# One level of Strassen for the second layer's input projection, with the weight sums made in DRAM

## The chip, the cores and the metric

One core of a Trainium2 chip. The metric is the device time of one execution in microseconds (us), the median of several runs. TensorE (PE) multiplies matrices, VectorE (DVE) and ScalarE (ACT) work elementwise, GpSimd (POOL) does a little of this and issues DMAs, SyncE (SP) issues most DMAs.

## The reference

Two residual layers over x of 512 tokens by 2048 columns, in float32:

```python
def hybrid_layer(x, ...):               # layer 0
    h = rms_norm(x, norm_g)
    aq, ak, av, agate, alog_in, bq, bk, bv, bgate = split_cols(h @ w_in, IN0_SIZES)
    ya = mixer_a(...)                   # gated delta rule in chunks of 64, both directions
    yb = mixer_b(bq, bk, bv, bgate, ...)  # attention with rotary positions
    return x + jnp.concatenate([ya, yb], axis=-1) @ w_out

def gmlp_layer(x, ...):                 # layer 1
    h = rms_norm(x, norm_g)
    u, v, gate = jnp.split(h @ w_in, 3, axis=-1)      # w_in is 2048 x 6144
    u = gelu(u)
    v = layer_norm(gelu(v), ln_g, ln_b)
    s = jnp.einsum('gts,bnsgc->bntgc', w_s, vc) + bias   # vc: v in 4 chunks, 16 column groups
    z = u * s * silu(gate)
    return x + z @ w_out
```

## The kernel before

Every large product is split into float32r parts: an operand is hi + lo, and a product is hi x hi + hi x lo + lo x hi, three matmuls into one PSUM bank. `proj` (L244) makes one group of up to 512 weight columns: 16 k-steps (128 rows of the weights each), in each of them four parts (blocks of 128 tokens or columns), in each part three matmuls. A part is a quarter-step below.

Weights come in slabs of 256 rows (512 KB) by `load_raw` (L213) on SP's queue into three buffers `raw`, and `split` (L222) makes hi on ScalarE (L230) and lo on VectorE (L231), two k-steps ahead of the matmuls that use them; a slab is asked for when the first half of the slab two before it is split, so it has four k-steps to land.

All engines run in the order in which the program is written out. That order comes from a small planner: `sub` (L170) is called once per quarter-step, counts the waits of side work down by `tick` and lets the lanes `front`, `back` and `side` write out pieces of their generators. A generator yields a positive number for VectorE time that it asks for, and a negative one for quarter-steps to wait. `force` runs the lanes until a named key is done. `spill` queues a store for some quarter-steps later. A group of 512 columns is 64 quarter-steps, one of 352 columns is counted as 44.

The groups in order: A2, K0, K1, Q0, Q1, V0, BQ0, V1, BQ1, BKV, A0, A1, BG0, BG1 (layer 0's input), O0 to O3 (its output), VV0 to VV3 (layer 1's v), GG0, UU0, ..., GG3, UU3 (gate and u), R0 to R3 (layer 1's output). Beside K0 to V1 runs `batch` (L530): it makes the decays, loads the gram blocks into M (six loads on POOL's queue, L629), inverts the triangular blocks of 32 in M and W on VectorE (L660 to L666), and hands the off-diagonal blocks to `merge` (L758), 256 small matmuls a direction, whose inputs go through DRAM (e_d, then eb) by POOL's queue. Four scattered stores (L703) put the diagonal blocks into u_d. `chunk_a` sets the key "A2" when the decayed query blocks are stored; then the recursion `scan` (L810) and `attention` start.

The last output group of layer 0 leaves x1; `h1_turn` (L1277) transposes it and makes h1 (hi and lo). The sums of squares become the row scale rs1, applied at evacuation. v stays in SBUF (vt), is normalised in place by `layer_norm1` (L1322), and `spatial` (L1359), one for each pair GGj, UUj, splits it by column groups, multiplies by the spatial weights, combines with u x gate and transposes to zT. `z_split` makes the output projection's operand of it.

## Time and profile before

| | |
|---|---|
| runs, median of 3 | 1748.71 us (1745.74 to 1748.79) |
| profiled execution: its time, its span | 1745.44 us, 1743.7 us |
| TensorE busy in the span | 1714.5 us (98%) |
| VectorE, ScalarE, POOL busy | 866.1, 698.4, 152.5 us |
| layer 1's input stage | 1002 to 1556 us |
| moved by DMA | 221 MB |

The busy time of TensorE is counted from the start of matmuls that overlap; a part without idle time is not a part at full speed, so the spacing of starts is read where a matmul's price is wanted.

### The profile page before, as it was taken

Reading aid. Unit: us, or ns where it says so; the run is one execution under the profiler, and the core shown is the slowest. Engines: PE = TensorE matmul, PEld = TensorE weight load, DVE = VectorE, ACT = ScalarE, POOL = GpSimd, SP = SyncE. Lnnn points to the kernel's source line nnn. Section 1 sums busy time; section 2 is a strip of 40 time slices with the busy share of each in tenths; the row PEclk is TensorE's granted clock in tenths of the full one; section 3 lists DMA queues with packets and bytes.
Section 4 is the critical chain, followed back from the end, with each engine's and each line's share of the span. In section 5 each row is a group of like instructions: output and inputs, shape, how many; then the busy total and the mean of one; then the engine's idle time right before and its main releaser. Section 6 shows DMA issues by size and latency. Waiting matters only on the chain.

```text
span 1743.7 us, 23347 instructions
## 1 busy us (share of the span) xinstructions
PE 1714.5 (98%) x8819; PEld 1402.7 (80%) x8819; DVE 866.1 (50%) x1570; ACT 698.4 (40%) x1423; POOL 152.5 (9%) x177
## 2 busy tenths in 40 slices
PE   9999999979999999999999999999999999999999
PEld 9877777757788997788788888888888888888887
DVE  4545588825765767875533333238342424245232
ACT  6443443514445555565532232223333433343221
POOL 0200200230001313440100000000000000000000
PEclk9999999989999999999999999999999999999999
DMA  6534544695556555435444453333333233333443
GB/s 199 134 103 124 125 121 104 160 185 141 144 141 172 158 145 178 129 105 169 151 133 129 128 166 97 90 92 107 98 91 90 81 96 92 96 115 113 134 139 103
DMA packets 166560, 221.36 MB, mean 127 GB/s; under 512 B 48545, under 2 KB 77521, under 8 KB 166448
## 3 DMA queue, kind: packets, MB, share of 16 engines
q1 hardware_dynamic: 161952, 207.27, 41.1%
q0 software_dynamic: 3744, 11.75, 3.2%
q8 instruction: 69, 1.13, 0.3%
q10 hardware_dynamic: 752, 0.86, 0.2%
q14 instruction: 43, 0.35, 0.1%
HBM read 186.18 MB, written 33.65 MB: 126 GB/s over the span
## 4 chain that ended last, share of the span: by engine, by line
PE 71%; ACT 3%; DVE 3%; issue 2%; DMA 2%; POOL 0%; SPq 0%; ACTq 0%; DVEq 0%
PE acc L276 19%; PE acc L275 19%; PE acc L277 19%; PE acc L271 2%; PE acc L273 2%; PE acc L272 2%; PE su L881 1%; PE sc L850 1%; DVE wlo L231 1%; PE sc L877 1%; ACT whi L230 1%; DMA eb<-e_d 1%; PE sc L863 1%; PE sc L851 1%; PE at L84 1%
## 5 line engine op out<-in xcount | busy, mean ns | idle before, releaser
L231 DVE TENSOR_TENSOR wlo<-raw,whi 128x512 fp32r<-128x512 f32 (+1 forms) x544 | 373.6, 687 | 747.8 <-ACT whi L230 740.2
L230 ACT CAST whi<-raw 128x512 fp32r<-128x512 f32 (+1 forms) x544 | 330.3, 608 | 724.8 <-PE acc L277 543.1
L275 PE MATMUL acc<-whi,h1h 128*128 128x512 f32 x768 | 304.5, 396 | 0.0
L277 PE MATMUL acc<-whi,h1l 128*128 128x512 f32 x768 | 303.3, 395 | 0.0
L276 PE MATMUL acc<-wlo,h1h 128*128 128x512 f32 x768 | 303.3, 395 | 0.0
L271 PE MATMUL acc<-hTh,whi 128*128 128x512 f32 x512 | 211.4, 413 | 0.9 <-DVE cs L509 0.9
L273 PE MATMUL acc<-hTh,wlo 128*128 128x512 f32 x512 | 203.2, 397 | 1.6 <-issue 1.6
L272 PE MATMUL acc<-hTl,whi 128*128 128x512 f32 x512 | 202.9, 396 | 0.0
L277 PEld LDWEIGHTS acc<-whi,h1l 128*128 128x128 f32 x768 | 143.9, 187 | 35.2
L275 PEld LDWEIGHTS acc<-whi,h1h 128*128 128x128 f32 x768 | 144.0, 187 | 34.8
L276 PEld LDWEIGHTS acc<-wlo,h1h 128*128 128x128 f32 x768 | 144.0, 188 | 34.5
L275 PE MATMUL acc<-whi,hTh 128*128 128x352 f32 (+1 forms) x384 | 160.7, 418 | 0.0
L277 PE MATMUL acc<-whi,hTl 128*128 128x352 f32 (+1 forms) x384 | 137.8, 359 | 0.2 <-DVE hTl L351 0.2
L276 PE MATMUL acc<-wlo,hTh 128*128 128x352 f32 (+1 forms) x384 | 137.9, 359 | 0.0
L273 PEld LDWEIGHTS acc<-hTh,wlo 128*128 128x128 f32 x512 | 96.5, 188 | 25.2 <-issue 2.0
L271 PEld LDWEIGHTS acc<-hTh,whi 128*128 128x128 f32 x512 | 96.8, 189 | 21.4 <-DVE cs L509 1.5
L272 PEld LDWEIGHTS acc<-hTl,whi 128*128 128x128 f32 x512 | 97.0, 190 | 18.6
L275 PE MATMUL acc<-whi,zh 128*128 128x512 f32 x224 | 87.2, 389 | 0.0
L276 PE MATMUL acc<-wlo,zh 128*128 128x512 f32 x224 | 86.9, 388 | 0.0
L277 PE MATMUL acc<-whi,zl 128*128 128x512 f32 x224 | 86.9, 388 | 0.0
L277 PEld LDWEIGHTS acc<-whi,hTl 128*128 128x128 f32 x384 | 72.1, 188 | 9.3 <-DVE hTl L351 0.5
L275 PEld LDWEIGHTS acc<-whi,hTh 128*128 128x128 f32 x384 | 72.8, 190 | 6.0 <-ACT hTh L350 0.3
(318 smaller groups left out, 2384.5 us busy)
## 6 DMA issues: line engine op xcount, KB each, us to landing
raw<-in_w_in_dram SPq DMA_DIRECT2D x184, 512.0 KB, 3.9
raw<-in_w_out_dram SPq DMA_DIRECT2D x64, 512.0 KB, 3.7
kv<-kv_d SPq DMA_DIRECT2D x32, 256.0 KB, 4.0
raw<-in_w_in_dram SPq DMA_DIRECT2D x22, 352.0 KB, 4.1
kv_d<-nat SPq DMA_DIRECT2D x16, 256.0 KB, 3.6
TA<-u_d SPq DMA_DIRECT2D x64, 64.0 KB, 3.0
o_d<-ob SPq DMA_DIRECT2D x32, 128.0 KB, 4.4
xr<-in_x_dram SPq DMA_DIRECT2D x16, 256.0 KB, 5.1
```

Of the source, the lines that this page charges most:

```text
L84: nc.tensor.transpose(out=o, in_=i, identity=ident[:k, :k])
L230: nc.scalar.copy(hi[:, :n], raw[:, a, :n])
L231: nc.vector.tensor_sub(lo[:, :n], raw[:, a, :n], hi[:, :n].bitcast(F32))
L271: mm(pt, lhsT=hi[:, s], rhs=ah, start=f, stop=False)
L272: mm(pt, lhsT=hi[:, s], rhs=al, start=False, stop=False)
L273: mm(pt, lhsT=lo[:, s], rhs=ah, start=False, stop=l)
L275: mm(pt, lhsT=ah[:, s], rhs=hi[:, cs], start=f, stop=False)
L276: mm(pt, lhsT=ah[:, s], rhs=lo[:, cs], start=False, stop=False)
L277: mm(pt, lhsT=al[:, s], rhs=hi[:, cs], start=False, stop=l)
L850: mm(pt[:, 0:128], lhsT=kq_chunk(h, cf), rhs=S[:, b, 0, :], start=True, stop=True)
L851: mm(pt[:, 128:256], lhsT=kq_chunk(h, cb), rhs=S[:, b, 1, :], start=True, stop=True)
L863: mm(pt[:, 256:384], lhsT=ta[:, 0, b, :], rhs=wk[:, 0, :], start=True, stop=True)
```

## The change

The twelve groups VV, GG and UU become six pairs of column groups (VV0 with VV2, VV1 with VV3, GGj with UUj). `fast` multiplies the 512 x 2048 operand by the 2048 x 1024 weights of a pair as 2 x 2 blocks with seven products (the Winograd form): P1 = A11 B11, P2 = A12 B21, P6 = S2 T2, N5 = Sa T1, P7 = S3 T3, Q4 = A22 T4, N3 = S4 B22. A product has 8 k-steps of two parts of three matmuls with 512 moving columns. The operand sums (S2, Sa, S3, S4) are made by VectorE in `h1_turn` and `mixes` from unsplit h1, then split by `halves2`. They lie in seven large buffers, so v and zT no longer fit; v goes to DRAM (v_d) and comes back by column group, where it is normalised (`v_norm`) right ahead of its split, and z of the first twelve groups goes through z_d.

The weight sums T1 to T4 (for v 1024 x 1024 each, for gate and u 1024 x 2048) are made in DRAM by `sums`, 128 rows at a time: plain transfers and adding transfers on POOL's queue, in a lane `mem` of their own, 5 quarter-steps after a move of 512 KB, 10 after one of 1 MB. After eight row blocks have been begun it waits for "A2".

In the pairs, a fourth hi/lo buffer (wx) lets a split run three k-steps ahead; from the second pair on a fourth slab buffer (in ex) lets a load run six k-steps ahead. The lane gives side work 0.27 us of VectorE per quarter-step. x1 is scaled by the first layer's row scale before the transposes (16 more operations on ScalarE in O0 to O3), with the epsilon of rs1 adjusted for it.

The merge's inputs lie in free parts of M and W, not in eb. The merges are put first in their lane; their loads come 2 quarter-steps earlier, their products start 14 after the last load, not 11; the four scattered stores of L703 come after the table transposes, 3 quarter-steps later. The recursion starts 12 quarter-steps after its first loads, not 15, and waits one less at a chunk's first and last step. x1's reload in the output groups is issued at the tenth k-step, not ahead of the group.

```diff
+    v_d = dr.tile([KT, P, NT, P], F32, name="v_d")
+    z_d = dr.tile([KT, P, T], F32, name="z_d")
+    HK = D // 2
+    tv_d = {q: dr.tile([HK, 1024], F32, name=f"tv{q}_d") for q in ("T1", "T2", "T3", "T4")}
+    tg_d = {q: dr.tile([HK, 2048], F32, name=f"tg{q}_d") for q in ("T1", "T2", "T3", "T4")}
...
+    FAST = ("P1", "P2", "P6", "N5", "P7", "Q4", "N3")
+    fasts = [("VV", j) for j in range(2)] + [("GU", j) for j in range(4)]
+
+    def quarters(kind, j):
+        c1, c2, t = (2048, 3072, tv_d) if kind == "VV" else (4096, 0, tg_d)
+        up, dn = slice(0, HK), slice(HK, D)
+        c = lambda c0: slice(c0 + j * 512, c0 + j * 512 + 512)
+        z = {q: t[q][:, j * 512:j * 512 + 512] for q in t}
+        z["B11"], z["B12"], z["B21"], z["B22"] = wi1[up, c(c1)], wi1[up, c(c2)], wi1[dn, c(c1)], wi1[dn, c(c2)]
+        return [z[q] for q in ("B11", "B21", "T2", "T1", "T3", "T4", "B22")]
+
+    slabs = [(g[1][q * 256:(q + 1) * 256, g[2]:g[2] + g[3]], g[3]) for g in groups for q in range(KT // 2)]
+    F0 = len(slabs)
+    slabs += [(z[q * 256:(q + 1) * 256, :], 512) for f in fasts for z in quarters(*f) for q in range(4)]
+    FR, F1 = F0 + 28, len(slabs)
...
     def load_raw(qi):
...
+        src, n = slabs[qi]
+        if FR <= qi < F1 and (qi - FR) % 4 == 3:
+            ex(0)
+            raw = ex_[0][:, 0:2, :]
+        else:
+            raw = sb.tile([P, 2, 512], F32, tag="raw", bufs=3, name=uid("raw"))
+        nc.sync.dma_start(raw[:, :, :n], src.rearrange("(a p) c -> p a c", p=P))
         raws[qi] = raw
 
     def split(i):
...
-        hi = sb.tile([P, 512], F32R, tag="whi", bufs=LOOK + 1, name=uid("whi"))
-        lo = sb.tile([P, 512], F32R, tag="wlo", bufs=LOOK + 1, name=uid("wlo"))
+        if F0 <= qi < F1 and (i - 2 * F0) % 4 == 3:
+            if not wx_:
+                wx_.extend(st("wx", [P, 512], F32R) for _ in range(2))
+            hi, lo = wx_
+        else:
+            hi = sb.tile([P, 512], F32R, tag="whi", bufs=LOOK + 1, name=uid("whi"))
+            lo = sb.tile([P, 512], F32R, tag="wlo", bufs=LOOK + 1, name=uid("wlo"))
         nc.scalar.copy(hi[:, :n], raw[:, a, :n])
         nc.vector.tensor_sub(lo[:, :n], raw[:, a, :n], hi[:, :n].bitcast(F32))
         splits[i] = (hi, lo)
         if a == 0:
             load_raw(qi + 2)
+            if FR + 3 <= qi + 3 < F1:
+                load_raw(qi + 3)
...
+    def fast(f, ops, evac, late=None, warms={}):
+
+        i0 = pos[0]
+        assert i0 == 2 * F0 + 56 * fasts.index(f)
+        home, todo = {}, []
+        for i in range(i0, i0 + 56):
+            o, k = FAST[(i - i0) // 8], (i - i0) % 8
+            for z in range(LOOK + 2):
+                if z < LOOK + 1 or i + z >= 2 * F0 + 3 and i + z < 2 * F1:
+                    split(i + z)
+            if k == 4 and o in warms:
+                warm(warms[o])
+            if k == 0 and o == "N3" and late is not None:
+                late()
+            if k == 0:
+                home[o] = [(chain if o[0] == "N" else acc)() for _ in range(2)]
+            hi, lo = splits[i]
+            a = ops(o, k)
+            for tb in range(2):
+                pt = home[o][tb]
+                ah, al = (a[:, w, tb * P:(tb + 1) * P] for w in range(2))
+                mm(pt, lhsT=ah, rhs=hi, start=k == 0, stop=False)
+                mm(pt, lhsT=ah, rhs=lo, start=False, stop=False)
+                mm(pt, lhsT=al, rhs=hi, start=False, stop=k == 7)
+                if tb == 0 and todo:
+                    evac(*todo.pop(0))
+                sub(1.0, 0.27)
+            splits.pop(i)
+            if k == 7:
+                todo.append((o, home[o]))
+        for z in todo:
+            evac(*z)
+        pos[0] = i0 + 56
...
+    def sums():
+
+        rows = [(t, n, c1, c2, q) for t, n, c1, c2 in ((tv_d, 1024, 2048, 3072), (tg_d, 2048, 4096, 0)) for q in range(8)]
+
+        def move(i, o, src, add):
+            t, n, c1, c2, q = rows[i]
+            rs = slice(q * P, (q + 1) * P)
+            if src in t:
+                s_ = t[src][rs, :]
+            else:
+                r0 = q * P + (HK if src[1] == "2" else 0)
+                c0 = c2 if src[2] == "2" else c1
+                s_ = wi1[r0:r0 + P, c0:c0 + n]
+            if add:
+                nc.gpsimd.dma_start(t[o][rs, :], s_, accum_op=ALU.add)
+            else:
+                nc.gpsimd.dma_start(t[o][rs, :], s_)
+            return n / 1024.0
+
+        STEPS = ((("T3", "B12", 0), ("T1", "B11", 0)), (("T3", "B22", 1), ("T1", "B12", 1)), (("T2", "T3", 0),),
+                 (("T2", "B11", 1),), (("T4", "T2", 0),), (("T4", "B21", 1),))
+        for n in range(len(rows) + len(STEPS) - 1):
+            if n == SUMS_STOP:
+                yield from until("A2")
+            for d, todo in enumerate(STEPS):
+                if 0 <= n - d < len(rows):
+                    for z in todo:
+                        yield -5.0 * move(n - d, *z)
+        done.add("sums")
+
+    SUMS_STOP = 8
...
-        eb = big("eb", [P, 8, 512])
-        back.add(merge(0, eb, um[f, 0:B, B:C]), True)
-        back.add(merge(1, eb, um[b, B:C, 0:B]), True)
+        fl = lambda t, z, q: t[:, z].rearrange("p a b -> p (a b)")[:, q * 512:q * 512 + 512]
+        back.add(merge(0, (fl(M, 2, 0), fl(M, 2, 1), fl(M, 3, 0)), um[f, 0:B, B:C]), True, True)
+        back.add(merge(1, (fl(W, 0, 0), fl(W, 0, 1), fl(W, 3, 0)), um[b, B:C, 0:B]), True, True)
...
     def merge(d, eb, dst):
 
-        yield -6
+        yield -4
         for w in (1, 0, 2):
             src = e_d[w, d * 64:d * 64 + 64, :].rearrange("q x -> (q x)").rearrange("(g p i) -> p g i", p=P, i=32)
-            nc.gpsimd.dma_start(eb[:, d * 3 + w, :].rearrange("p (g i) -> p g i", i=32), src)
+            nc.gpsimd.dma_start(eb[w].rearrange("p (g i) -> p g i", i=32), src)
             yield -2
-        yield -11
-        src = eb[:, d * 3 + 1, :]
+        yield -14
...
+            xs.append(st("xs", [P, 512]))
+            nc.scalar.activation(xs[t], z, AF.Copy, scale=sc1[:, t:t + 1])
             jk = st("jk", [P, 512])
-            nc.scalar.activation(jk, z, AF.Square, accum_out=ss1[:, t, j:j + 1])
+            nc.scalar.activation(jk, xs[t], AF.Square, accum_out=ss1[:, t, j:j + 1])
...
+    def halves2(nm, p, src):
+        z = op(nm, p)
+        nc.scalar.copy(z[:, 0], src)
+        nc.vector.tensor_sub(z[:, 1], src, z[:, 0].bitcast(F32))
...
+    def mixes():
+
+        def both(p):
+            h = hdn[p - p % 2][:, p % 2, :]
+            return hup[0][:, p, 0:256], hup[0][:, p, 256:512], h[:, 0:256], h[:, 256:512]
+
+        def mix(p, n):
+            a11, a21, a12, a22 = both(p)
+            s = m4("mix", [P, 4, 256])
+            nc.vector.tensor_sub(s[:, 0], a21, a22)
+            nc.vector.tensor_sub(s[:, 1], s[:, 0], a11)
+            return s
+
+        for p in range(8):
+            s = mix(p, 2)
+            yield 0.8
+            halves2("S2", p, s[:, 1])
+            done.add(("S2", p))
+            yield 0.5
...
+        for p in range(8):
+            s = mix(p, 3)
+            nc.vector.tensor_add(s[:, 2], both(p)[2], s[:, 1])
+            yield 1.2
+            halves2("S4", p, s[:, 2])
+            done.add(("S4", p))
+            yield 0.5
...
+        def f(o, banks):
+            if o == "P1":
+                into("X", banks)
+            elif o == "P2":
+                out("11", banks, "X", ALU.add)
+            elif o == "P6":
+                into("U2", banks, "X")
+            elif o == "N5":
+                t["N5"] = banks
+                t["Y"] = [st("pp", [P, 512]) for _ in range(2)]
+                for tb in range(2):
+                    nc.vector.tensor_tensor(t["Y"][tb], banks[tb], t["U2"][tb], op=ALU.subtract)
+            elif o == "P7":
+                into("U3", banks, "U2")
+                out("22", t["N5"], "U3", ALU.subtract)
+            elif o == "Q4":
+                out("21", banks, "U3", ALU.add)
+            else:
+                out("12", banks, "Y", ALU.add)
...
+        def v_load(a):
+            z = g4(ex(5 + a % 2))
+            nc.sync.dma_start(z, v_d[j * 4 + a])
+            return z
+
+        def v_norm(a):
+            for n in range(NT):
+                nc.vector.tensor_scalar(vr[:, n, :], vr[:, n, :], mv[:, 0, n:n + 1], mv[:, 3, n:n + 1],
+                                        ALU.subtract, ALU.mult)
+            yield 0.9
+            for z, f in zip(lg, (ALU.mult, ALU.add)):
+                nc.vector.tensor_tensor(vr, vr, z[:, a * P:(a + 1) * P].unsqueeze(1).to_broadcast([P, NT, P]), op=f)
+                yield 0.7
...
+        fast(("GU", j), act1, combine(take_gu(sgs, us)), late=z_first if j == 3 else None,
+             warms={"P2": AF.Silu, "P7": AF.Gelu, "Q4": AF.Silu, "N3": AF.Gelu})
```

## Rows read from the trace of the kernel before

**Rows 1.** Part 1 of the page: busy us, share of the span, instructions.

```profile
PE 1714.5 (98%) x8819; PEld 1402.7 (80%) x8819; DVE 866.1 (50%) x1570; ACT 698.4 (40%) x1423; POOL 152.5 (9%) x177
```

**Rows 2.** Busy time by stage; the first line names the columns.

```profile
core 0: us, PE busy (x) PEld busy (x) DVE busy (x) ACT busy (x) POOL busy (x), PEclk, DMA share, GB/s
49.00:218.00 169.00, 168.86 (x853) 134.86 (x852) 88.89 (x147) 67.52 (x114) 15.43 (x13) 1.00 0.48 121
...
392.00:822.00 430.00, 420.12 (x2332) 356.81 (x2331) 286.59 (x647) 231.34 (x613) 87.28 (x99) 1.00 0.51 149
822.00:1002.00 180.00, 177.70 (x799) 142.45 (x798) 70.51 (x105) 66.07 (x123) 5.18 (x4) 1.00 0.43 133
1002.00:1556.00 554.00, 554.00 (x2417) 445.88 (x2416) 201.08 (x307) 184.20 (x310) 8.70 (x13) 1.00 0.34 101
```

**Rows 3.** The layer's operand on TensorE: ns minimum/median/maximum, first and last start.

```profile
L275 PE MATMUL acc<-whi,h1h x768: 392/396/481, 1002.0 to 1555.5; 128*128 128x512 f32 x192
```

**Rows 4.** Timeline of TensorE: start us, duration us.

```profile
1059.76 0.40 PE L275 MATMUL acc<-whi,h1h 128*128 128x512 f32 x1
...
1060.46 0.39 PE L275 MATMUL acc<-whi,h1h 128*128 128x512 f32 x1
```

**Rows 5.** Busy time of the stretch with the merge, columns as in rows 2.

```profile
350.00:400.00 50.00, 39.73 (x639) 30.09 (x638) 13.67 (x16) 8.96 (x15) 16.86 (x19) 0.90 0.89 178
```

**Rows 6.** Groups by line, 1002 to 1556 us: count | busy us, mean ns | idle before.

```profile
L231 DVE TENSOR_TENSOR wlo<-raw,whi 128x512 fp32r<-128x512 f32 x192 | 132.7, 691 | 329.9 <-ACT whi L230 329.3
L230 ACT CAST whi<-raw 128x512 fp32r<-128x512 f32 x192 | 119.0, 620 | 341.4 <-PE acc L277 339.2 <-DVE vt L1339 2.2
L242 ACT ACT_TABLE_LOAD x9 | 11.5, 1283 | 0.2
L1409 DVE SCALAR_TENSOR_TENSOR u<-sp,cols,u 128x256 f32<-128x256 f32 x24 | 10.5, 479 | 11.7 <-PE sp L1406 11.6
L1337 DVE TENSOR_TENSOR vt<-vt,lg 128x1024 f32<-128x1024 f32 x8 | 9.8, 1223 | 0.2
L1384 DVE TENSOR_TENSOR vl<-vt,vh 128x256 fp32r<-128x256 f32 x24 | 9.0, 416 | 0.0
L1383 ACT CAST vh<-vt 128x256 fp32r<-128x256 f32 x24 | 8.6, 406 | 0.0
L1335 DVE TENSOR_SCALAR vt<-vt,mv 128x1024 f32<-128x1024 f32 x8 | 6.5, 810 | 2.0 <-POOL mv L81 2.0
```

**Rows 7.** DMA engines, first 49 us in 40 slices: busy tenths, GB/s.

```profile
DMA  0389999999999999970037073027404820491099
GB/s 0 95 192 332 340 302 284 322 323 310 355 378 401 386 393 360 345 237 25 0 45 249 0 187 114 0 23 252 166 0 42 296 90 0 55 333 40 0 77 365
```

**Rows 8.** DMA issues: queue, count, KB each, median us from issue to landing.

```profile
raw<-in_w_in_dram SPq DMA_DIRECT2D x184, 512.0 KB, 3.9
...
x_d<-xr SPq DMA_DIRECT2D x16, 256.0 KB, 5.0
```

**Rows 9.** Timeline: the recursion's first loads on SP's queue.

```profile
391.66 1.29 SPq L834 DMA_DIRECT2D TA<-u_d  x2
```

**Rows 10.** Timeline of ScalarE: the two first reads of M's blocks.

```profile
219.49 0.26 ACT L633 ACTIVATE bsA<-M 128x32 f32<-128x32 f32 x1
219.90 0.26 ACT L633 ACTIVATE bsA<-M 128x32 f32<-128x32 f32 x1 [0.15 <-DMA M<-g_d]
```

**Rows 11.** TensorE's waits, 340 to 400 us: total us, times, longest.

```profile
PE mg L773 <- DMA eb<-e_d: 7.1, 2, 5.8
```

**Rows 12.** Timeline of POOL around the loads of eb.

```profile
335.93 1.10 POOL L703 DMA_DIRECT2D u_d<-W  x1
...
349.90 6.88 POOL L763 DMA_DIRECT2D eb<-e_d  x6 [9.62 <-issue]
```

**Rows 13.** Busy time of the output stage's first 34 us, columns as in rows 2.

```profile
1556.00:1590.00 34.00, 34.00 (x159) 27.69 (x158) 23.39 (x43) 19.60 (x40) 0.00 (x0) 1.00 0.29 83
```

More of the change, by code (lines that the diff above doesn't have):

```diff
@@ L245, in proj @@
         i0 = pos[0]
-        nm, _, _, n, tr = groups[i0 // KT]
-        assert nm == name, (nm, name)
+        _, _, _, n, tr = next(g for g in groups if g[0] == name)
         banks = [acc() for _ in range(4)]
@@ L1225, in encoder @@
     back.add(batch(), True)
+    mem.add(sums())
     proj("K0", act0, evac_conv("k", 0))
@@ new lines, in h1_turn @@
+        if j == 3:
+            yield from until("O3")
+            yield from mixes()
+    def mixes():
[13 more added lines that the diff above has]
+            done.add(("S2", p))
+            yield 0.5
+        for p in range(8):
+            s = mix(p, 3)
+            yield 0.8
+            halves2("Sa", p, s[:, 0])
+            done.add(("Sa", p))
+            yield 0.5
+        for p in range(8):
+            halves2("A22", p, both(p)[3])
+            done.add(("A22", p))
+            yield 0.5
+        for p in range(8):
+            s = mix(p, 3)
+            nc.vector.tensor_add(s[:, 2], both(p)[2], s[:, 1])
+            yield 1.2
+            halves2("S4", p, s[:, 2])
+            done.add(("S4", p))
+            yield 0.5
@@ new lines, in encoder, with z_home @@
+    for j in range(2):
+        fast(("VV", j), act1, combine(take_v(j)), warms={"P1": AF.Gelu} if j == 0 else {})
+    stored("v1")
+    front.add(layer_norm1())
+    z_h, z_l, zs = [], [], {}
+    def z_home(k):
+        if k in zs:
+            return zs[k]
+        if k < 2:
+            if 0 not in zs:
+                z = [m4("z01", [P, 2, T], F32R) for _ in range(2)]
+                zs[0], zs[1] = ((y[:, 0, :], y[:, 1, :]) for y in z)
+        else:
+            i, j = divmod(k - 2, 8)
+            while len(z_h) <= i:
+                z_h.append(big("zh", [P, 8, T], F32R))
+                z_l.append(big("zl", [P, 8, T], F32R))
+            zs[k] = z_h[i][:, j, :], z_l[i][:, j, :]
+        return zs[k]
@@ L1472, in tail @@
             eng.dma_start(out2[t * P:(t + 1) * P, j * 512 + c:j * 512 + c + 256], z)
-        proj(f"R{j}", actz, evac, tail=tail if j == 3 else None)
+        proj(f"R{j}", actz, evac, late=load, tail=tail if j == 3 else None)
     for j in range(4):
```

314 lines of the change are left out of this document (183 added, 131 removed).

## The prediction

> **What bounds the kernel now.** I read the page's first part: TensorE's matmul row is busy 1714.5 of 1743.7 us, every other engine half or less [rows 1]. Then the busy times by stage: in the second layer's input stage, 1002 to 1556 us, TensorE is busy in all 554.0 us at clock 1.00, while VectorE works 201 us, ScalarE 184 us and the DMA engines show 0.34 at 101 GB/s [rows 2]. So there a matmul that is removed is time removed, until something else takes its place. The row of the second layer's operand says that its 768 matmuls per kind (three kinds, 2304 in all) fill just this stage [rows 3], and two starts of the same kind lie 0.70 us apart with three matmuls in between, 0.2333 us each [rows 4]. 2304 x 0.2333 = 537.5 us; the other 16.5 us of the stage are transposes and the spatial matmuls, which stay. Most of the remaining idle time of TensorE is in one place: 350 to 400 us has 10.3 us idle and clock 0.90 [rows 5], the merge.
>
> **Gross gain.** Two column groups of 512 take 2 x 192 matmuls now. One level of Strassen takes 7 products x 8 k-steps x 2 row blocks x 3 = 336. Six pairs: 288 matmuls fewer, x 0.2333 = **-67.2 us**. The moving side stays 512 wide, so a matmul keeps its price.
>
> **What each pair now asks.** A k-step has 6 matmuls (1.40 us), not 12 (2.80), and still needs one weight split: ScalarE 0.620 us and VectorE 0.691 us [rows 6]. Weights per pair go from 32 to 56 k-steps of 256 KB, 14.7 MB in 78.4 us (336 x 0.2333): 187 GB/s, where 101 flow now [rows 2]. With the spill of v and z (some 2 MB a pair) about 215 GB/s. The DMA engines reach 300 to 400 GB/s where they show 9 tenths at the start [rows 7]; I take 350. So the steady pair isn't bound by DMA. Loads land in 3.9 us [rows 8] and are issued six k-steps (8.4 us) ahead with the fourth buffer, four (5.6 us) in the first pair, where that buffer isn't there yet.
>
> VectorE in a G/U pair: 56 x 0.691 = 38.7; 14 PSUM combinations, priced like a split, 9.7; spatial work 2 x 1.22 for u x gate, 4 x (4 small normalisations, at 0.81 / 8 = 0.1 up to 0.42 each, I take 0.25, + 2 x 0.69), 4 x 0.69 and 0.69 for splits, 8 x 0.48: 19.2 [rows 6]. Sum 67.6 of 78.4 us. ScalarE: 56 x 0.62 = 34.7, ten evacuations at 0.7, four table loads at 1.28, the rest 6: 53. Both fit, but VectorE at 86% delivers late now and then, and spatial's matmuls stand in TensorE's queue in order. Below zero is excluded, as only waits can be added; above, a k-step late by 1 us at half of the 16 spatial steps is 8 us. For the three G/U pairs that carry a spatial pass I take **+6** (0 to 20) in all. The normalisation in place that went (24 operations of 0.8 to 1.2 us) was hidden: nothing gained.
>
> **The first pair.** All operands are made here. VectorE: 38.7 for splits; S2, Sa, A22, S4 are 3, 3, 1 and 4 operations of 256 columns per block, 11 x 8 x 0.416 = 36.6; four A12 remainders 1.7; 12 combinations 8.3. That is 85 us beside 80 of matmuls and transposes. Besides, the lane gives VectorE 0.27 us a quarter-step, 112 of them make 30 us, so 15 or so of the 24 mixed operands of S2, Sa and S4 are made only when TensorE asks; there VectorE waits for ScalarE's 0.406 us copy and a hand-over, about 0.6 us, in its own queue: 9 us. 94 against 80: **+14 us** (5 to 25). Late is then the operand, at S2, Sa and S4's products. The weights must pass in the same stretch with a shorter lead; if sums and weights crowd each other there, the stall is largely the same one; I allow +1 more, **+15**.
>
> **The sums.** Four tables of 4 + 8 MiB, each one plain transfer and one adding transfer: 50.3 MB copied, 50.3 MB added, in 128 moves. They are paced in quarter-steps, 5 per 512 KB. 48 moves run from 49 us for 240 quarter-steps (0.70 us, to about 218), then they stop until "A2" (the recursion's first load, 391.7 us, comes right behind it [rows 9]; quarter-step 456) and need 16 x 5 + 64 x 10 = 720. From "A2" to the first pair there are 636 of 1092 in all, counted from 64 a group (44 for 352 columns). So they run 84 quarter-steps into the first pair. First use of the wide tables is the third product of the first G/U pair, 260 quarter-steps after VV0's start: some 120 us of slack. No row shows a DRAM-to-DRAM or an adding transfer. 50.3 MB at 350 GB/s is 144 us of all engines: a load's price, the lower bound for a copy (and for an add). A store of 256 KB to DRAM takes 5.0 us to land where a load of 512 KB takes 3.9 [rows 8], so a copy, that does both, may cost two loads, and an add, that reads its target too, three: 288 to 720 us in all. I take 1.5 loads for a copy (rows of 4 and 8 KB are longer than either) and 2.5 for an add: 216 + 360 = 576. Room in their stretches: 169 x (1 - 121/350) + 430 x (1 - 149/350) + 180 x (1 - 133/350) + the first pair 80 x (1 - 214/350) = 111 + 247 + 112 + 31 = 500 us [rows 2], and 120 x 0.39 = 47 more until first use: 547. So they fill the DMA engines and overrun by some 29 us. Weights keep part of their share; what they lose reaches TensorE in three places. (a) The first pair and the next, with the sums' tail beside weights of 187 GB/s. (b) The groups before: their lead of four k-steps is 11 us against 3.9 now. (c) POOL's queue is in order and its transfers follow one another in it: M's six loads stand behind copies. ScalarE already waits for their landing (0.15 us) [rows 10], with its weight casts behind that; two splits, 5.6 us, are made ahead. Also behind POOL's waits for a copy are the rope operations and reciprocal roots; an add comes some nine moves (9 x 3.5 us) after its copy, so this hurts only with a lag above 30 us. I take **+20**, most of the overrun (0 to 720 - 547 = 173).
>
> The Trainium skill, "DMA: Bandwidth & Descriptors", section "Latency and other measured facts", gives 207 to 214 GB/s for copies between HBM tensors; an estimate from it is 240 us for my copies, near their upper bound. "Collectives: The Full Stack", section "The bandwidth ceiling", says that an adding transfer reads two sources and ran at half a copy's rate; no run here shows either yet. By the two the sums would need an estimated 240 + 480 = 720 us, the upper bound, and the choking rival below would be the outcome.
>
> **Merge.** POOL's four scattered stores go out at 335.9 to 340.3, then POOL waits 9.6 us before the loads of eb; TensorE waits 7.1 us for these [rows 11, 12], and a mean clock of 0.90 over 50 us is 10 us at 1.2 GHz, so 5 us lost [rows 5]. The change issues the six loads ahead of the stores and starts the products 24 instead of 23 quarter-steps after. Gain between 0 and 7.1 + 5 = 12 us: I take **-8**. The stores come 3 quarter-steps after the table transposes; the recursion's first loads on SP wait for them, covered by the 12 quarter-steps kept. Scan's shorter gaps: 0 (+-2).
>
> **R0.** In its first 34 us VectorE works 23.4 [rows 13]. Normalisation of the last spatial pass adds 4 x (4 x 0.25 + 2 x 0.69) = 9.5, two late z splits 1.4: 34.3 of 34. z blocks 12 to 15 are then forced; z 2 to 11 come back by SP, two blocks (5.6 us) ahead of need against some 4 us. SP's weight loads stand behind these. **+5** (0 to 15). ScalarE's 16 scalings in the O stage (0.69 each) lie beside its 66 of 180 us: nothing.
>
> **Sum** against the profiled execution's own 1745.4: -67.2 + 6 + 15 + 20 - 8 + 5 = -29.2, 1716. The median of the runs shown is 3 us above the profiled one, their lowest beside it; half of this on top gives **1718 us**.
>
> **Rivals.** *Whole gain*: sums and mixed operands hide. 1745.4 - 67.2 - 8 + 10 = 1680 to 1695. For it: long rows, an add at a copy's price (288 us in 547); against: 85 us of VectorE in 80. Chance 0.14. *VectorE or the hi/lo buffers bind in every pair*: a lead of three k-steps is 4.2 us, and a burst of four combinations with two normalisations is about that; 5 us on each of the five other pairs in place of the 6 gives 1718 + 19 = 1737, up to 1750. Against: 67.6 of 78.4 us. Chance 0.13. *Sums choke the DMA engines* (slower): a copy costs two loads, an add 2.5; 648 us, 101 over the room, in place of the 20: 1718 + 81 = 1799 (1755 to 1830). The place is the weight loads from 392 us to the second pair. It decides once the sums need more than some 547 + 20 + 30 = 597 us, since 30 us is all that the forecast gains. For it: the room is full by my own count; against: the tables' first use can wait, and sums that are late only run on. Chance 0.25.
>
> **Numbers.** Forecast 1700 to 1735, chance 0.48. The range leaves out the best of the whole gain and the worse half of the choking: 1682 to 1785. 0.2% is 3.5 us, what a measurement of this kernel can tell. Faster: 0.48 + 0.14 + 0.10; same 0.03; slower 0.25.
>
> **What would show it.** Input stage of 2016 matmuls of 0.233 us; gaps of TensorE in the first pair released by VectorE's operand remainders, few in the other pairs; the DMA share between 49 and 218 us near 0.9; M's landing later than 219.9 us; no wait of the merge for eb; sums ending between 1065 and 1180 us. Wrong if weight casts wait for raw loads over whole stages, if matmul spacing changes, or if POOL's rope operations wait for copies.

## The result: the profile after, and where the time went

The changed kernel takes 1920.8 us (median of 4 runs, 1917.1 to 1924.7) against 1748.0 before: ratio 1.099, 95% interval 1.097 to 1.101. It is 173 us slower, where 30 us less were forecast. The time lies above the forecast's range, and above that of every rival.

The page's first part and its DMA queues (packets, MB, share of 16 engines' span): TensorE's matmul row, 98% before [rows 1], is at 89%, and GpSimd's queue q0 now carries 111 MB, where it carried 11.75. SP's loads and stores, the weights among them, go through q1.

```profile
PE 1705.8 (89%) x8531; PEld 1378.0 (72%) x8531; DVE 1054.4 (55%) x1958; ACT 823.8 (43%) x1647; POOL 240.2 (12%) x303
q1 hardware_dynamic: 197856, 260.75, 45.1%
q0 software_dynamic: 18336, 111.37, 23.1%
```

The windows of the kernel after, columns as in [rows 2]. TensorE has gaps in a few stretches, the longest of 44 us, and there the granted clock falls well below 1.00 (0.57 is a mean of 1.00 and 0.50, that is of 2.4 and 1.2 GHz), the DMA engines are nearly full or full (0.83 to 1.03), and ScalarE and VectorE do little. Between these stretches (750 to 800) and behind them (1650 to 1700) it is busy throughout.

```profile
50.00:100.00 50.00, 42.81 (x176) 33.75 (x175) 18.85 (x44) 15.39 (x27) 13.49 (x19) 0.90 0.83 223
450.00:500.00 50.00, 10.34 (x38) 8.26 (x38) 1.19 (x4) 3.90 (x11) 4.90 (x8) 0.57 1.03 256
750.00:800.00 50.00, 49.49 (x263) 41.04 (x263) 37.27 (x72) 33.16 (x84) 25.53 (x28) 1.00 0.86 243
950.00:1000.00 50.00, 24.59 (x86) 17.41 (x84) 5.36 (x8) 8.06 (x16) 6.49 (x9) 0.69 1.02 275
1000.00:1050.00 50.00, 27.04 (x80) 19.33 (x80) 8.99 (x18) 9.00 (x18) 3.46 (x5) 0.74 1.02 260
1650.00:1700.00 50.00, 50.00 (x223) 40.40 (x222) 40.37 (x76) 28.05 (x46) 0.00 (x0) 1.00 0.65 209
```

What TensorE and ScalarE wait for in the bad stretches is loads on SP's queue, most of them weights. The first fence has two rows of ScalarE's waits over the whole span (us in all, times, longest), the second what crossed the DMA engines between 950 and 1050 us (queues as above; then issues: count, KB each, median us from issue to landing). A weight load of 512 KB lands in 51.8 us, where it took 3.9 [rows 8].

```profile
ACT whi L262 <- DMA raw<-in_w_in_dram: 120.7, 16, 21.1
ACT whi L262 <- DMA raw<-in_w_out_dram: 64.2, 7, 17.8
```

```profile
q0 software_dynamic: 2285, 22.32, 87.9%
q1 hardware_dynamic: 2354, 4.42, 13.9%
tgT_d<-in_w_in_dram POOLq DMA_DIRECT2D x9, 1024.0 KB, 38.0
raw<-in_w_out_dram SPq DMA_DIRECT2D x6, 512.0 KB, 51.8
x_d<-xr SPq DMA_DIRECT2D x4, 256.0 KB, 63.2
```

Between 420 and 505 us it isn't only weights. TensorE's longest wait of all, 44.2 us, is for VectorE, which waits there for the recursion's keys (kv). These come by SP's queue as well, and SP takes 17.4 us to issue two loads of TA, 1.29 before [rows 9]. From 418.2 to 471.6 us it issues no weight load.

```profile
PE sc L969 <- DVE wk L954: 44.2, 1, 44.2
DVE wk L954 <- DMA kv<-kv_d: 34.8, 1, 34.8
449.06 17.43 SPq L940 DMA_DIRECT2D TA<-u_d  x2
```

Between 950 and 1050 us the two queues sent about as many packets each, but a packet of q0 has 9.8 KB and one of q1 (the weights) 1.9 KB. Between 450 and 471 us, where q1 carries the recursion's short rows, the counts are equal almost to the packet, and the bytes stand 12 to 1:

```profile
q0 software_dynamic: 790, 5.29, 94.6%
q1 hardware_dynamic: 788, 0.45, 9.0%
```

The timeline of GpSimd shows how the sums' moves came there (start, duration, line, transfer): nine in the first six us, the rest as earlier ones land, with nothing of TensorE in between.

```profile
939.83 1.28 POOL L1277 TENSOR_TENSOR ybTl<-yo,ybTh 128x512 fp32r<-128x512 f32 x1 [3.86 <-ACT ybTh L1274]
941.05 0.53 POOL L385 DMA_DIRECT2D tgT_d<-in_w_in_dram  x1
941.57 1.72 POOL L383 DMA_DIRECT2D tgT_d<-in_w_in_dram  x2
942.66 1.15 POOL L385 DMA_DIRECT2D tgT_d<-tgT_d  x1
...
944.74 1.80 POOL L385 DMA_DIRECT2D tgT_d<-in_w_in_dram  x1
947.04 0.54 POOL L385 DMA_DIRECT2D tgT_d<-in_w_in_dram  x1 [0.50 <-DMA tgT_d<-in_w_in_dram]
954.24 0.84 POOL L383 DMA_DIRECT2D tgT_d<-in_w_in_dram  x1 [6.66 <-DMA tgT_d<-in_w_in_dram]
```

Between such bursts GpSimd waits long, at the next operation that needs another engine (three of its waits, whole span):

```profile
POOL att L1075 <- PE su L987: 185.8, 1, 185.8
POOL rs L81 <- DVE sm L1479: 153.1, 1, 153.1
POOL M L736 <- PE acc L306: 80.3, 1, 80.3
```

By the timeline of GpSimd there are four bursts with 96 of the 128 moves: 52 to 158 us (42 of the 48 moves that the forecast spread over 49 to 218; the other six go out at 245 to 251, behind the loads of M), 421 to 472, 941 to 1030 and 1185 to 1216. Set against the version without these transfers (e1 below), by the starts of the same weight casts in ScalarE's timeline, the changed kernel loses 31 us in the first, 61 in the second, 72 in the third, 28 in the fourth with the rest of the first pair, 10 elsewhere: 202 us between the profiled executions.

### The profile page after: what moved, and what is told of

It reads as the page before. It is cut to its first block, busy times and chain, and to the rows that moved or that the text cites. A ratio compares the mean times of both kernels' runs of the same rounds, so it can differ in the third digit from the quotient of the medians.

```text
span 1922.9 us, 23978 instructions
## 1 busy us (share of the span) xinstructions
PE 1705.8 (89%) x8531; PEld 1378.0 (72%) x8531; DVE 1054.4 (55%) x1958; ACT 823.8 (43%) x1647; POOL 240.2 (12%) x303
## 3 DMA queue, kind: packets, MB, share of 16 engines
q0 software_dynamic: 18336, 111.37, 23.1%
## 5 line engine op out<-in xcount | busy, mean ns | idle before, releaser
L263 DVE TENSOR_TENSOR wlo<-raw,whi 128x512 fp32r<-128x512 f32 (+1 forms) x569 | 395.2, 698 | 641.2 <-ACT whi L262 625.2
L262 ACT CAST whi<-raw 128x512 fp32r<-128x512 f32 (+1 forms) x569 | 342.2, 607 | 626.9 <-PE acc L310 183.8
L304 PE MATMUL acc<-hTh,whi 128*128 128x512 f32 x512 | 217.4, 425 | 12.4 <-ACT whi L262 10.3
L306 PE MATMUL acc<-hTh,wlo 128*128 128x512 f32 x512 | 207.3, 405 | 3.5 <-DVE wlo L263 1.9
L305 PE MATMUL acc<-hTl,whi 128*128 128x512 f32 x512 | 207.4, 405 | 0.0
L304 PEld LDWEIGHTS acc<-hTh,whi 128*128 128x128 f32 x512 | 99.7, 195 | 34.6 <-ACT whi L262 11.2
L356 PE MATMUL acc<-whi,opA 128*128 128x512 f32 x216 | 89.2, 413 | 23.0 <-ACT whi L262 23.0
L308 PE MATMUL acc<-whi,yaT 128*128 128x512 f32 x128 | 57.0, 445 | 39.2 <-DVE xr L1376 20.4
L357 PE MATMUL acc<-wlo,opA 128*128 128x512 f32 x216 | 88.8, 411 | 0.5 <-DVE wlo L263 0.4
L358 PE MATMUL acc<-whi,opA 128*128 128x512 f32 x216 | 87.9, 407 | 0.0
L309 PEld LDWEIGHTS acc<-wlo,hTh 128*128 128x128 f32 x384 | 72.8, 190 | 5.2
L551 DVE SCALAR_TENSOR_TENSOR cv<-cs,taps,cv 128x510 f32<-128x510 f32 (+1 forms) x96 | 71.4, 745 | 0.8 <-ACT cv L546 0.4
## 6 DMA issues: line engine op xcount, KB each, us to landing
tgT_d<-in_w_in_dram POOLq DMA_DIRECT2D x48, 1024.0 KB, 18.7
```

Of the source, the lines that this page charges most:

```text
L262: nc.scalar.copy(hi[:, :n], raw[:, a, :n])
L263: nc.vector.tensor_sub(lo[:, :n], raw[:, a, :n], hi[:, :n].bitcast(F32))
L304: mm(pt, lhsT=hi[:, s], rhs=ah, start=f, stop=False)
L305: mm(pt, lhsT=hi[:, s], rhs=al, start=False, stop=False)
L306: mm(pt, lhsT=lo[:, s], rhs=ah, start=False, stop=l)
L308: mm(pt, lhsT=ah[:, s], rhs=hi[:, cs], start=f, stop=False)
```

## The experiments

Theory A: the planner's quarter-steps set only the order of instructions. A move waits for nothing of TensorE, so GpSimd runs ahead of it to its next wait on another engine and issues all moves in between as a burst. Rival B: the total of the traffic, adds above all, is too much wherever it lies. Rival C: it is the length of the rows, as the queues are served a packet each in turn. Rival D: the paired stage itself costs it. All times are medians; the interval is that of the ratio to the kernel before on the same chip. Of each diff only the lines that matter are shown; "..." marks what is left out.

| run | us | 95% interval |
|---|---|---|
| after | 1920.8 | 1.097 to 1.101 |
| e1 no sums | 1724.8 | 0.985 to 0.988 |
| e2 copies only | 1856.3 | 1.060 to 1.064 |
| e3 before + sums | 1918.5 | 1.096 to 1.099 |
| e4 tied | 1768.6 | 1.010 to 1.014 |
| e5 short rows | 1797.0 | 1.027 to 1.031 |
| e6 tied, short | 1759.4 | 1.004 to 1.008 |
| e7 merge alone, in before | 1738.2 | 0.994 to 0.996 |
| e8 tied, moved | 1762.0 | 1.005 to 1.010 |
| e9 tied, short, moved | 1752.1 | 1.001 to 1.003 |
| e10 no sums, scan as before | 1718.3 | 0.982 to 0.985 |
| e11 no sums, early operands | 1706.1 | 0.975 to 0.978 |
| e12 G/U pairs only | 1730.9 | 0.989 to 0.993 |
| e13 e9 with copies only | 1741.9 | 0.995 to 0.999 |
| e14, e15 G/U, earlier stop | 1740.3, 1739.0 | 0.995 to 0.998, 0.994 to 0.997 |
| e16 G/U, earlier stop, quicker | 1730.9 | 0.989 to 0.992 |

**e1, no sums.**

```diff
-    mem.add(sums())
+    z["T1"], z["T2"], z["T3"], z["T4"] = z["B12"], z["B11"], z["B22"], z["B21"]
```

> The changed kernel without the transfers that make the weight sums: the pairs read plain blocks of the weights where they read sums (this leaves the sums out of the computation). All else stands. Theory A (the sums' transfers, issued in bursts by GpSimd, crowd out the weight loads; the paired stage itself costs what was forecast) expects 1695 to 1715 us, which is the forecast without its term for the sums. Theory D (the paired stage with its operands and evictions is itself the loss) expects over 1800 us.

1724.8 us: the sums' transfers cost 196 us, and D falls as the main cause. But the time is above A's 1715 as well. Where that comes from, e7, e10 and e11 show.

**e2, copies only.**

```diff
-                nc.gpsimd.dma_start(t[o][rs, :], s_, accum_op=ALU.add)
+                nc.gpsimd.dma_start(t[o][rs, :], s_)
```

> Every adding transfer is a plain copy of the same blocks (this leaves the additions out of the sums). Count, size, order and moment of the transfers stand; only the reading of the second operand and the add fall away. By the forecast's estimate (a copy 1.5, an add 2.5 loads) the work of the transfers falls to 0.71. Theory A (bursts of any traffic of that kind) expects 1840 to 1890 us. Theory B (adding transfers are the price, plain ones would be hidden) expects under 1790 us.

1856.3: as A said. The adds' second read is worth 64 of 196 us; 132 stay with plain copies. In the second burst TensorE is busy for 15.65 of 50 us all the same:

```profile
400.00:450.00 50.00, 15.65 (x76) 12.45 (x77) 3.13 (x6) 4.04 (x8) 18.14 (x32) 0.66 1.00 315
```

The q0 row of e2 gives the moves' price as well:

```profile
q0 software_dynamic: 18336, 111.37, 18.1%
```

Without sums (e1) q0 has 10.70 MB and 3.3% of 1720.4 us, 57 us. With copies only 18.1% of 1853.4 is 335 us: 278 for 100.7 MB, 362 GB/s. In the changed kernel 23.1% of 1922.9 is 444: 387 for the same moves, so the 50.3 MB of adds take 248 us, 203 GB/s, 1.8 times a copy. These are sums of the packets' own times beside other traffic; no run has the moves alone.

**e3, the sums in the kernel before.** Its diff is the sums' lane alone, as in the change.

```diff
+    mem.add(sums())
```

> The kernel before with the sums' transfers added at the places that the change gives them; nobody reads the sums (the second layer works as before). Theory A expects the loss of the sums as in the changed kernel: 130 to 220 us over before, that is 1880 to 1970 us, in the same three stretches (50 to 160, 420 to 520, and the last one after the scan). Theory D (the paired stage is the loss) expects under 1800 us.

1918.5, 171 us over before, with the second layer untouched. The loss isn't that of the pairs. It stands in the same stretches:

```profile
450.00:500.00 50.00, 8.00 (x29) 6.64 (x30) 5.65 (x10) 5.52 (x14) 3.76 (x6) 0.53 0.90 246
1000.00:1050.00 50.00, 21.79 (x69) 16.12 (x68) 2.59 (x4) 2.28 (x4) 3.45 (x5) 0.67 1.04 275
```

**e4, tied.** The decisive one: same moves, same bytes, but GpSimd can't run ahead.

```diff
...
+            nc.vector.memset(mk, 0.0)            # mk: a column of its own for each move
+            nc.gpsimd.tensor_copy(mkj, mk)
...
```

> The changed kernel; before each of the sums' transfers VectorE writes a one-column marker at the place in its own order where the planner put the transfer, and GpSimd copies the marker and only then issues the transfer, so that GpSimd can't run ahead of the weight splits and so of TensorE. Amount and kind of the transfers stand. Theory A (the bunching is the loss) expects 1715 to 1775 us and no stretch of more than 10 us in which GpSimd issues over five transfers. Theory B (the total of the traffic is the loss) expects over 1850 us.

1768.6: 152 of 196 us are gone, and B with them as the main cause. In GpSimd's timeline each move now waits for VectorE's marker, 4 to 8 us apart; at most five go out in any 10 us, where the changed kernel sent up to eleven. In the window from 950 to 1000 us the DMA engines are nearly as full as in the burst (0.98), and TensorE is busy for 48.55 us, not 24.59.

```profile
956.67 0.18 POOL L387 COPY mkj<-mks 128x1 f32<-128x1 f32 x1 [7.59 <-DVE mks L386]
957.10 0.52 POOL L391 DMA_DIRECT2D tgT_d<-tgT_d  x1 [0.25 <-issue]
960.79 0.18 POOL L387 COPY mkj<-mks 128x1 f32<-128x1 f32 x1 [3.17 <-DVE mks L386]
961.22 0.81 POOL L389 DMA_DIRECT2D tgT_d<-in_w_in_dram  x1 [0.24 <-issue]
```

```profile
950.00:1000.00 50.00, 48.55 (x220) 38.95 (x220) 18.93 (x40) 22.64 (x44) 5.39 (x12) 1.00 0.98 257
```

**e5 and e6, short rows**, untied and tied. Plain and adding transfers are split alike.

```diff
...
-            nc.gpsimd.dma_start(t[o][rs, :], s_)
+            for x in range(0, n, 512):
...
+                nc.gpsimd.dma_start(t[o][rs, x:x + 512], s_[:, x:x + 512])
```

> The changed kernel, untied: each of the sums' transfers is cut into transfers of 512 columns, so that its rows are of 2 KB, as the weight loads' are, where they were of 4 and 8 KB. Bytes, order and place stand; GpSimd issues two or four times as many. Theory C (the queues are served a packet each in turn, so the longer rows take the DMA engines from the weights) expects 1750 to 1830 us and weight loads that land in under 20 us in the bursts. Theory A without C (it is the amount in the burst, whatever the length of the rows) expects 1880 to 1930 us.

> The tied version, its transfers cut to 512 columns as well. If the length of the rows still costs once the transfers are spread, 1748 to 1762 us; if spreading alone was what mattered, 1764 to 1774 us as the tied version; if the larger number of transfers costs, over 1774 us.

1797.0 (e5): C is right too. The bursts stay, yet 124 of 196 us go. Between 950 and 1050 us of e5 the packets are again about one to one, but now so are the bytes. A weight load lands in 14.2 us: more than the four k-steps of its lead (11.2), but less than these and the two by which a split runs ahead (16.8), and TensorE is busy with the DMA engines at 1.09:

```profile
q0 software_dynamic: 6637, 14.40, 64.7%
q1 hardware_dynamic: 7422, 14.02, 41.5%
raw<-in_w_out_dram SPq DMA_DIRECT2D x14, 512.0 KB, 14.2
```

```profile
950.00:1000.00 50.00, 48.56 (x217) 38.87 (x216) 18.83 (x33) 20.21 (x41) 19.37 (x28) 1.00 1.09 274
```

By the casts of e5 and e1, of the 71 us that stay 9 stand in the first burst, 32 in the second and 26 in the first pair; where the changed kernel lost 72, e5 loses next to nothing. Tied and short together (1759.4) take 9 us less than tied alone. So most of the 196 us needs both, burst and long rows; taking away either removes most. The Trainium skill, "DMA: Bandwidth & Descriptors", section "Queues, rings and completion order", says that a DMA engine goes round the queues it has work for, a packet at a time. By that rule the share of a queue in bytes goes with its packets' size; the rows agree, 790 to 788, 2285 to 2354 and 6637 to 7422 packets. The page's packet is a bundle of descriptors; that the profile counts the same thing isn't shown. I had not weighed it.

**e7, the merge alone.** The merge's blocks in M and W and its order, put into the kernel before.

```diff
...
-        eb = big("eb", [P, 8, 512])
...
+        back.add(merge(0, (fl(M, 2, 0), fl(M, 2, 1), fl(M, 3, 0)), um[f, 0:B, B:C]), True, True)
...
```

> The kernel before with one part of the change alone: the merge's blocks in M and W, the merges first in their lane, the stores of the diagonal blocks behind the transposes. The forecast's term for this part (minus 8 us) expects 1738 to 1742 us. The version without sums was 7 us late against the kernel before when the second layer began, and 5.6 us of that stood there at the first weight cast behind the merge; if this part is why, 1752 to 1757 us.

1738.2, 9.4 us less than before: the forecast's term, and not the reason for e1's late start. TensorE's waits at the merge (340 to 400 us), 7.1 before [rows 11]:

```profile
PE mg L772 <- DMA M<-e_d: 2.3, 1, 2.3
PE mg L772 <- DMA W<-e_d: 1.2, 1, 1.2
```

**e10, the scan.** e1 with the scan's pacing as in the kernel before.

```diff
-        yield -12
+        yield -15
...
```

> The version without the sums' transfers, its scan paced by the lines of the kernel before (initial wait of 15 instead of 12 quarter-steps, the full waits between steps). The merge alone gave 9.4 us, yet the version without sums stood 1.5 us behind the kernel before at the last stage ahead of the O groups. If the scan's earlier start takes the 9 us (a first wait for the keys' load of 5 us and a lower clock), 1712 to 1719 us; if not, 1722 to 1728 us.

1718.3, 6.5 less than e1. The scan's shorter gaps were not free: TensorE's wait for the keys' load (5.0 us, in e1's waits below) is not among e10's.

**e11, operands.** e1, with the products of S2, Sa, A22 and S4 multiplying operands that are long there.

```diff
-        return op(USES[o], p)
+        return op({"S2": "A11", "Sa": "A12", "A22": "S3", "S4": "A12"}.get(USES[o], USES[o]), p)
```

> The version without the sums' transfers; four of a pair's seven products multiply operands that are long there (A11, S3, A12) where they multiplied S2, Sa, A22 and S4, which are still made, in the same order, and read by nobody (this leaves those operands out of the computation). If the first pair's 106 us against 83 in the others are TensorE waiting for those operands, 1703 to 1712 us and a first pair of 85 to 95 us; if they are ScalarE and VectorE being full of the making of them, so that weight casts come late, 1718 to 1726 us and a first pair of over 100 us.

1706.1, 18.7 less. Shown are TensorE's waits in e1 over the whole span, then the windows of the first and second pair of e1 and of e11, each from TensorE's first matmul of the pair to that of the next. (From first weight cast to first weight cast the first pair takes 106.5 us in e1 and 90.0 in e11; but the casts run up to three k-steps ahead, and part of e1's stall at S4's product falls behind the next pair's first cast.) The two pairs take 188.6 us in e1 and 172.6 in e11, with VectorE as busy (134.4, 132.9 us). So the wait for operands cost 16 us. Another 14 stay above the 80 us that I gave the first pair without waits and the 78.6 of the second; what of that is the work of making the operands isn't shown.

```profile
PE chain L357 <- ACT opSa L1396: 6.4, 6, 1.1
PE chain L357 <- ACT opS L1396: 6.2, 5, 2.0
PE aux L84 <- ACT xs L1379: 5.8, 8, 1.0
PE sc L970 <- DMA kv<-kv_d: 5.0, 1, 5.0
```

```profile
1009.50:1119.50 110.00, 92.22 (x354) 64.81 (x353) 81.36 (x167) 59.00 (x119) 1.01 (x1) 0.95 0.56 164
1119.50:1198.10 78.60, 78.58 (x338) 62.99 (x337) 53.07 (x83) 39.73 (x66) 0.00 (x0) 1.00 0.71 213
```

```profile
1009.80:1097.40 87.60, 83.97 (x354) 63.57 (x352) 74.10 (x155) 56.31 (x116) 1.01 (x1) 1.00 0.65 195
1097.40:1182.40 85.00, 81.15 (x338) 63.88 (x337) 58.81 (x96) 41.28 (x70) 0.00 (x0) 0.98 0.68 208
```

**e8 and e9, moved.** e8 is e4 with the start 48 quarter-steps later and the stop two rows of blocks later; e9 is e6 with that start, the stop one row later and its end later, and the scan as before.

```diff
+        yield -48
-    SUMS_STOP = 8
+    SUMS_STOP = 9      # e8: 10
+                yield -60      # e9, behind until("A2")
```

> The tied version with its transfers begun 48 quarter-steps later (some 33 us, behind the loads and stores of the first stages) and the stop moved two rows of blocks later, so that some of the second set's transfers lie in the emptier stretch between 218 and 340 us. Theory A (what is left of the tied version's loss against the version without sums, 44 us, is DMA engines that are full in some stretches) expects 1740 to 1762 us. Theory B (the total of the traffic decides) expects 1765 to 1775 us.

> A version built from what the runs so far say: tied, transfers of 512 columns, begun 48 quarter-steps later, the stop one row of blocks later and its end 60 quarter-steps later (so that little runs beside the merge, 345 to 430 us), and the scan's pacing lines as in the kernel before. By sums: the tied short version's 1759, less 6 (the first stages), 5 (the merge's stretch), 6 (the tail that lies in the first pair) and 9 (the scan) is 1733; expected 1726 to 1744 us. If the merge's stretch or the scan were no cost, 1745 to 1755 us.

e8 takes 1762.0 us, 7 below e4, at the edge of what was expected; the first stages lose nothing now, but its moves ran on into the merge's stretch. e9 takes 1752.1 and misses its range: it is 34 us over its version without sums (e10). It lies where it was expected if the merge's stretch or the scan were no cost, but e10 shows that the scan is one. By the casts of e9 and e10, 3 of the 34 us stand at the end of the merge, 17 come between 550 and 870 us, 14 in the first two pairs.

**e13, e9 with copies only**, the edit of e2.

> The tied, short, spread version (1752 us), every adding transfer a plain copy (this leaves the additions out of the sums). Count, markers and GpSimd's issues stand; only the adds' second read falls away. What is left of the sums' cost there is 34 us over the version without sums (1718 us). If DMA engines that are too full cause it (theory B on what is left), 1722 to 1738 us; if GpSimd's time for three times as many issues and markers does, which rope and attention wait for, 1744 to 1754 us.

1741.9, between the two expected ranges: 10 of the 34 us are the adds' second read. That decides nothing on the other 24. By their pages q0's packets, less those of e10, take 450 us in e9 and 309 in e13, 31% less, and 10 is 30% of 34. So a loss in proportion to the traffic (B on what is left) fits, and so does a part that is GpSimd's time.

**e12, only the G/U pairs.** The v groups are four plain products again, operands A11, A21, A12, A22; S3 is made behind them. The sums left, two thirds of the moves, are tied and in rows of 512 columns, begun 48 quarter-steps later, with the stop at the fifth row of blocks, 60 quarter-steps more behind the stop and a slower pace (7 and, behind the stop, 10 quarter-steps for 512 KB, not 5). The scan is as before.

```diff
-    for j in range(2):
-        fast(("VV", j), act1, combine(take_v(j)), warms={"P1": AF.Gelu} if j == 0 else {})
+    for j in range(4):
+        proj(f"VV{j}", act_vv, evac_v(j), func=AF.Gelu if j == 0 else None)
...
```

> A version that keeps the change where the runs show a gain: the first four column groups of the second layer (v) as four plain products of 192 matmuls, as in the kernel before, and only the four G/U pairs by Strassen; their sums (two thirds of the transfers) tied, in rows of 512 columns, 24 before the merge's stretch and the rest from behind it up to some 1000 us; the scan's lines as before, the merge as changed. All is computed. Worked out from runs: kernel before 1748, merge -9, the four G/U pairs -44 (329.5 us of the version without sums against 373.2), the O groups' evictions +6, the last groups' extra loads +4, the sums +5 to +20 gives 1710 to 1725 us. If the operands' making is as dear here as in the first v pair (23 us more), 1730 to 1748 us.

1730.9, faster than both kernels, 6 above the range's end. It lies in the range of the rival (1730 to 1748), but not for the rival's reason: its first pair shows no wait for operands and takes 81.6 us, cast to cast; the four pairs together take 331.7 us, where the kernel before needs 373 for the eight groups. So the pairs pay where operands lie ready. One wait stands out, that of TensorE for the merge's small loads behind the sums:

```profile
PE mg L890 <- DMA W<-e_d: 10.1, 1, 10.1
```

**e14, e15 and e16, an earlier stop.** e14 stops the moves one row of blocks earlier; e15 has rows of 4 KB besides; e16 is e15 with a quicker pace behind the stop. In e14 and e15 the last sums end so late that loads of the first pair are issued ahead of them and read sums that are not complete.

```diff
-    SUMS_STOP = 5
+    SUMS_STOP = 4
...
-                        yield -(10.0 if n >= SUMS_STOP else 7.0) * move(n - d, *z)
+                        yield -(7.5 if n >= SUMS_STOP else 7.0) * move(n - d, *z)      # e16
```

> The version with only the G/U pairs, the stop one row of blocks earlier, so that no sums' transfer is under way when the merge's blocks are fetched (there TensorE waited 10.1 us for W). If that wait goes and the rest stands, 1716 to 1725 us; if the transfers that are put later cost as much there, 1727 to 1735 us.

> The same with the sums' transfers in rows of 1024 columns (4 KB) where they had 512 (2 KB): half as many transfers for GpSimd to issue, each row twice as long. If what is left of the sums' cost is GpSimd's time (its issues and markers ahead of rope and attention), 3 to 8 us less than the version beside it; if longer rows still cost the weight loads where the DMA engines are 0.75 to 0.85 busy, as much or more.

> The version with only the G/U pairs, in rows of 1024 columns, the stop at the fourth row of blocks, and a quicker pace behind the stop (15 instead of 20 quarter-steps for 1 MB), so that the sums end before the first pair's loads; all is computed. From the version with the stop at the fifth row (1731 us): less 10 (the merge's wait); the sums end near 1100 us and the first pair has its 81.6 us. 1716 to 1726 us; if the quicker pace costs more beside the attention, 1727 to 1735 us.

In all three the wait for W is gone. e14 (1740.3) misses both its ranges, as the time is given back and more in the first pair, which takes 94 us, and 97 in e15. Half the issues in rows twice as long (e15 against e14) make no difference that the intervals tell. e16 has its 81.6 us in the first pair again. Its profiled span is 8.7 us below that of e12, but it was its fastest execution and the other one of e12's slower, and the medians are equal: the gain isn't shown.

## Why the prediction was wrong, point by point

**The step that failed** is in "The sums": "They are paced in quarter-steps, 5 per 512 KB. 48 moves run from 49 us for 240 quarter-steps". I took the place in the program for the time of issue. A lane's quarter-step is time only for an instruction that waits for TensorE, directly or through its engine's queue; I even wrote that POOL's "transfers follow one another" and never asked what else holds POOL back. e4 shows it: the same moves, held to the quarter-steps, cost 44 us, not 196 (1768.6 and 1920.8 against 1724.8).

**A second step** failed beside it: "Weights keep part of their share". The forecast never asked how large a part, and it counted the sums' long rows as an advantage. e5 shows the reverse: with rows as short as the weights' the same bursts cost 72 us, not 196.

**The size of the sums** was wrong in the other direction. I forecast 216 + 360 = 576 us of all engines against room for 547; the rows give 139 + 248 = 387. By my own account they fitted with 160 us to spare, and the choking rival, whose point was 597 us, would have been out. An account by stages of what fits says nothing on a burst of 90 us in which one queue takes 88% of the engines. e3's 171 us in a kernel that reads no sum says the same.

**The choking rival** (1799, "the place is the weight loads from 392 us to the second pair") had the right victim for the most part, the weight loads, and three of four places. It missed the first burst (31 us), the recursion's loads in the second and the cause, so its price for the sums, 20 + 81 us, was half of the 196, and its range ended at 1830. By the two pages of the Trainium skill that I set beside it I had an estimate of 720 us for the sums. The 207 to 214 GB/s of the Trainium skill, "DMA: Bandwidth & Descriptors", section "Latency and other measured facts", measured there with rows of 16 KiB, don't hold for these copies in rows of 4 and 8 KB, which took the engines' time of 362; that an add runs at half a copy's rate (the Trainium skill, "Collectives: The Full Stack", section "The bandwidth ceiling") is near the 203 measured. They pointed to the outcome, but not to its reason; a forecast by them would have been right in direction, by luck.

**The lead**: "their lead of four k-steps is 11 us against 3.9 now". The second number failed, with 51.8 us in the third burst; in the second, SP's queue stood at the recursion's loads, and for 53 us no weight load was issued. With 14.2 us in e5 TensorE still had its weights (busy for 48.56 of 50 us).

**Gross gain** holds, and **the steady pairs** cost less than the +6: the four G/U pairs take 329.4 us without sums against 373.2 for the groups before, cast to cast, 43.8 less, of 44.8 by 48 matmuls a pair x 0.2333. The second v pair takes 78.6 us, where two groups took 89.6, and so gave all of its 11. That is +1.

**The first pair** was +15 and is +30 (110.0 against 80). The mechanism, operands made only when asked for, is right for 16 of the 30 by e11; the other 14 are open.

**Merge** -8: -9.4 measured. **R0** +5: from the first cast of the last groups to the end of the span 197.0 us (e1) against 192.9, +4.

**Left out**: the scan's shorter gaps "0 (+-2)" cost 6.5 us (e10), and the O groups' extra scalings, "nothing", cost 5.8, as the transposes wait for them (the row on xs). With the 10 us by which the pairs together were short (15 in the first, less 5 in the others) these are 22 of the 27 us by which e1 stands above the forecast without its sums (1718 less 20).

**The signs**: matmul spacing held (78.6 us for the 336 matmuls of e1's second pair, 0.234 each). The DMA share from 49 to 218 us was 0.84, near the 0.9 that I had named, and M's loads, issued from 238.4 us on, landed later: both fit a burst as well as a spread, so they told nothing; 0.94 to 158 us and 0.67 behind would have. The sums' last move was issued at 1215 us, not by 1180. What I named as proof of an error, weight casts that wait for raw loads over whole stages, is what the waits show; between 600 and 905 us no operation of GpSimd's rope and attention waited for a move.

**What stays open**: the 24 us that the tied, short, moved sums cost beyond the adds' second read (e9, e13). GpSimd's time (88.2 busy us between 700 and 870 in e9, 46.4 in e10) and full DMA engines for small transfers are both possible; e13 and e15 didn't tell them apart. Open too are the 14 us of the first pair.

## What to carry to other kernels

A planner's due time binds a transfer only if the transfer waits for something that the paced engine does: tie background moves to that engine's progress (a one-column marker was enough), or they go out in a burst. Ask of a new stream of transfers not only what it takes of the engines in all, but which queue it shares them with packet by packet, and cut its rows to the length of those that mustn't wait. And do the new scheme where its operands lie ready: the G/U pairs alone, with their sums tied, ran at 0.991 of the kernel before.

## What the runs showed of the hardware that I had not expected

- Where GpSimd's and SP's queues both had work, they sent about a packet each, whatever its size: 790 and 788 packets with 5.29 and 0.45 MB (450 to 471 us), 2285 and 2354 with 22.3 and 4.4 MB (950 to 1050 us), and 6637 and 7422 with 14.4 and 14.0 MB when the rows were equal (e5).
- DRAM-to-DRAM copies in rows of 4 and 8 KB took the engines' time of 362 GB/s, no more than I had assumed for a load; adding transfers took that of 203 GB/s.
- DMA engines that are full by the profile (0.98 in e4, 1.09 in e5) hardly stalled TensorE where a weight load landed in 7.1 and 14.2 us: it was busy for 48.6 of 50 us in both.
